# A hybrid decoder layer on one core: both token blocks of the first sub-layer multiplied before their norm factor is known

## The chip, the cores and the metric

The kernel is one program on one core of a Trainium2 chip. It has TensorE (PE, matrix products), VectorE (DVE), ScalarE (ACT), GpSimd (POOL) and SyncE (SP), each working through its own instructions in order, and DMA queues that bring data from memory. The metric is the device time of one execution in microseconds (us). The time before is the median of 3 runs, 754.89 us (753.69 to 754.94).

## The reference, cut to what matters

The layer is a SwiGLU feed-forward, a pair of token mixers and another feed-forward, each with a norm before and behind it. The change is in the first norm and in the first products that follow it:

```python
def rmsnorm(x, g):
    y = x * lax.rsqrt(jnp.mean(x * x, axis=-1, keepdims=True) + EPS)
    return y * g

def swiglu(x, w_gate, w_up, w_down):
    return (jax.nn.silu(x @ w_gate) * (x @ w_up)) @ w_down

h = x                                     # (1, 256, 1024) float32
h = h + 0.5 * rmsnorm(swiglu(rmsnorm(h, ffn1_pre_g), ffn1_w_gate, ffn1_w_up, ffn1_w_down), ffn1_post_g)
...                                       # mixers, second feed-forward
```

The norm's factor r = rsqrt(mean(x²) + eps) is one number per token. So (x·r·g) @ W = r·((x·g) @ W): the product can be made of x·g alone and multiplied by r behind it.

## The kernel before, in words

**Tiles.** The 256 tokens are two blocks of 128, block 0 and block 1; `h[:, b, halves[q]]` is half q (512 channels) of block b. Every float32 operand is split into a high part (rounded to the matrix unit's float32r) and a low remainder, and a product takes three matmuls: high·high, low·high, high·low. ACT makes the high part (for weights the cast at L167) and DVE the remainder (L168). Weights come in chunks of 1 MB, `raw`, three buffers deep (`RAW_BUFS`), loaded from SP by `load_to` (L140). `split_steps` (L150) makes `whi` and `wlo` of a chunk in two halves, then asks for a later chunk. The first feed-forward's chunks 0 and 1 are the first 512 columns of the gate weights (channels 0 to 511 and 512 to 1023), chunks 2 and 3 the same of the up weights; from chunk 4 on, 256 columns each are taken with the weights as the moving side, and both blocks at once (`mm_w`, L206).

**The opening.** `Norm.products` (L484) takes the first four chunks with the tokens standing: one token block, one chunk, 12 matmuls of 512 columns (`mm_nat`, L222), so 8 such sets, 96 matmuls. A set needs the block's activations turned to channels on partitions: PE transposes four 128x128 pieces into `pu` (`turn`, L336), ACT writes the high part times the gain (L343), DVE the remainder (L345).

- Block 0 is turned without r (`raw_u`), since r0 isn't known yet. Its products get r0 at their eviction (L527, L531), and `rescale` (L513) later makes r0·u for the rest of the sub-layer: `rescaled` (L381) spreads r0 over the partitions with a matmul of `ones` by a diagonal (`rb`, L385; the diagonal is made by POOL, L378), ACT copies it (`rbs`, L387), DVE multiplies `pu` by it (`us`, L392, 8 instructions), ACT and DVE split the result (L191, L192).
- Block 1 is normed first: DVE makes its sums of squares (L364), POOL its factor r1 (L330, L331) and x·r1 (`un`, L373), and PE turns that (`turn1`). Its products need no factor.

**Order.** Up to the end of `products` the order on PE, ACT, DVE and SP is that of the program text (`own_order(PE, ACT, DVE, SP)`, L264; POOL follows its own text). What stands between two sets is in the table `at` (L610): a number n names what is issued after the n-th set. The sets run block 0 on chunks 0 and 1, block 1 on chunks 0 and 1, block 0 on 2 and 3, block 1 on 2 and 3. `more` takes one more chunk, that is, it puts that chunk's four splitting instructions into ACT's and DVE's queues; `settle` issues the evictions held back; `rescale` stands after set 5. `norm.turns1` (block 1's turning) stands after set 1. The transposition of the block's gated product (`back`, L533) goes after set 7 for block 0 and behind set 8 for block 1. SP issues the four quarter-loads of x (256 KB each), then chunk 0 in four pieces, chunks 1 and 2 in two each, and each later chunk when a `raw` buffer is free. `warm(n)` (L291) issues n idle matmuls; 6 stand at the very start and 8 (`FILL`) ahead of the first set.

Of the kernel before, what the change touches and what calls it, by code (L numbers as in the profile page):

```python
# [36 lines left out]
RAW_BUFS = 3  # L37
AHEAD = 3
WARM = 6
FILL = 8  # L40
TAIL = 3
BG_US = 3.15
GATE_US = 1.35
# [5 lines left out]
def tile_hybrid_layer(ctx: ExitStack, tc: tile.TileContext, x, ffn1_pre_g, ffn1_w_gate, ffn1_w_up,  # L49
# [10 lines left out]
    def k4(shape, name, dt=F32):  # L60
        return sb.tile(shape, dt, tag="k4", name=name, bufs=K4_BUFS)
# [13 lines left out]
    def pj(name):  # L75

        return ps.tile([P, 512], F32, tag="pj", name=name, bufs=3)
# [62 lines left out]
    def load_to(n):  # L140
        while len(raws) < min(n, len(chunks)):
            i = len(raws)
            src, shape = chunks[i]
            r = sb.tile(shape, F32, tag="raw", name=f"raw{i}", bufs=RAW_BUFS)
            nj = shape[1] // 4 if i == 0 else shape[1] // 2 if i < 4 else shape[1]
            for j in range(0, shape[1], nj):
                nc.sync.dma_start(r[:, j:j + nj, :], src[:, j:j + nj, :])
            raws.append(r)

    def split_steps(ahead=True):  # L150


        i = len(splits)
        load_to(i + 1)
        r, shape = raws[i], chunks[i][1]
        nj = shape[1] // 2
        his, los = [], []
        splits.append((his, los))
        for q in range(2):
            hi = k4([P, nj, shape[2]], f"whi{i}{q}", F32R)  # L160
            lo = k4([P, nj, shape[2]], f"wlo{i}{q}", F32R)
            his.append(hi)
            los.append(lo)
            n = 1 if i == 0 else nj
            for j in range(0, nj, n):
                js = slice(j, j + n)
                nc.scalar.copy(hi[:, js, :], r[:, q * nj + j:q * nj + j + n, :])  # L167
                nc.vector.tensor_sub(lo[:, js, :], r[:, q * nj + j:q * nj + j + n, :], hi[:, js, :].bitcast(F32))  # L168
                yield
        raws[i] = None  # L170
        if ahead:
            load_to(i + 1 + RAW_BUFS)
# [7 lines left out]
    def take(ahead=AHEAD):  # L180

        i = taken[0]
        taken[0] += 1
        split_to(i + ahead)
        his, los = splits[i]
        splits[i] = None
        nj = chunks[i][1][1] // 2
        return (lambda j: his[j // nj][:, j % nj, :], lambda j: los[j // nj][:, j % nj, :])

    def split(hi, lo, src):  # L190
        nc.scalar.copy(hi, src)  # L191
        nc.vector.tensor_sub(lo, src, hi.bitcast(F32))  # L192
# [26 lines left out]
            nc.scalar.copy(dst[:, m, :], acc[:, T:])  # L219
            nc.vector.tensor_tensor(dst[:, m, :], acc[:, :T], dst[:, m, :], ALU.add)  # L220

    def mm_nat(acc, w, act, k0, first, last, late):  # L222


        (wh, wl), (ah, al) = w, act
        pairs = [(ah, wh), (al, wh), (ah, wl)] if late == "w" else [(ah, wh), (ah, wl), (al, wh)]
        terms = [(p, j) for j in range(4) for p in pairs[:2]] if late == "w" else \
            [(p, j) for p in pairs[:2] for j in range(4)]
        terms += [(pairs[2], j) for j in range(4)]
        for i, ((a, b), j) in enumerate(terms):  # L230
            nc.tensor.matmul(acc, a(k0 + j), b(j), start=first and i == 0, stop=last and i == 11)  # L231


    act_since, act_fence = [], [None]
# [37 lines left out]
    for b in range(2):  # L272
        for q in range(2):
            nc.sync.dma_start(h[:, b, halves[q]], xv[:, b, halves[q]])
    load_to(RAW_BUFS)
    act_table(SILU)

    ident = const.tile([P, P], F32, name="ident")
# [54 lines left out]
        return r  # L333

    last_pool = [None]
    def turn(b, q, src, g, to, name):  # L336

        pu = bg([P, 4, P], f"pu_{name}{b}{q}")
        for i in range(4):
            nc.tensor.transpose(pu[:, i, :], src[:, i * P:(i + 1) * P], ident)  # L340
        hi, lo = to(q)
        for i in range(4):
            nc.scalar.activation(hi[:, i, :], pu[:, i, :], AF.Identity, scale=g(q * 4 + i))  # L343
        for i in range(4):
            nc.vector.scalar_tensor_tensor(lo[:, i, :], pu[:, i, :], g(q * 4 + i), hi[:, i, :].bitcast(F32),  # L345
                                           ALU.mult, ALU.subtract)
        return pu

    def in_u(b):
        bs = slice(b * P, (b + 1) * P)  # L350
        return lambda q: (uT[q][:, :, 0, bs], uT[q][:, :, 1, bs])

    def of_block(to):

        parts = [to(q) for q in range(2)]
        return lambda j: parts[j // 4][0][:, j % 4, :], lambda j: parts[j // 4][1][:, j % 4, :]

    def rms(b, tag, eng=None):

        ss = tiny(2, f"ss_{tag}{b}")  # L360
        for q in range(2):
            src = h[:, b, halves[q]]
            if eng is nc.vector:
                nc.vector.scalar_tensor_tensor(jk([P, 512], f"sq_{tag}{b}{q}"), src, 1.0 / D, src, ALU.mult,  # L364
                                               ALU.mult, accum_out=ss[:, q:q + 1])
            else:
                sum_sq(ss[:, q:q + 1], src, 1.0, f"sq_{tag}{b}{q}")
        return rstd_of(ss, 1.0, f"r_{tag}{b}")

    def unit(b, q, r, tag, eng):  # L370

        un = k2([P, 512], f"un_{tag}{b}{q}")
        eng.tensor_scalar(un, h[:, b, halves[q]], r, None, ALU.mult)  # L373
        return un

    def diag(r, tag):
        dr = k2([P, P], f"dr_{tag}")
        last_pool[0] = nc.gpsimd.tensor_scalar(dr, ident, r, None, ALU.mult).ins  # L378
        return dr

    def rescaled(pus, r, g, tag, dr):  # L381

        dr = diag(r, tag) if dr is None else dr
        rb = bg([P, P], f"rb_{tag}")
        nc.tensor.matmul(rb, ones, dr, start=True, stop=True)  # L385
        rbs = k2([P, P], f"rbs_{tag}")
        nc.scalar.copy(rbs, rb)  # L387
        out = []
        for q in range(2):
            us = k2([P, 4, P], f"us_{tag}{q}")  # L390
            for i in range(4):
                nc.vector.scalar_tensor_tensor(us[:, i, :], pus[q][:, i, :], g(q * 4 + i), rbs, ALU.mult,  # L392
                                               ALU.mult)
            out.append(us)
        return out

    def set_u(us):
        for q in range(2):
            split(*in_u(0)(q), us[q])

    def post_norm(b, acc, pg, fold, tag):

# [55 lines left out]
    class Norm:  # L458

        def __init__(self, tag, g):
            self.tag, self.g, self.pus = tag, g, []
            new_u(tag)
            self.to0 = in_u(0)
            self.dr = None
            self.left = []

        def block0(self):
            for q in range(2):  # L470
                self.turn0(q)
            self.r0 = rms(0, self.tag)

        def turn0(self, q):
            self.pus.append(turn(0, q, h[:, 0, halves[q]], self.g, self.to0, self.tag))

        def unit1(self, engs=(nc.vector, nc.vector)):
            r = rms(1, self.tag)
            self.un = [unit(1, q, r, self.tag, engs[q]) for q in range(2)]

        def turn1(self, q):
            turn(1, q, self.un[q], self.g, in_u(1), self.tag)

        def products(self, ws, evict, at, turns=((0, 0), (0, 1), (1, 0), (1, 1)), late="u"):  # L484

            n = 0
            for b, i in turns:
                act = of_block(self.to0 if b == 0 else in_u(1))  # L490
                acc = pj(f"pn_{self.tag}{b}{i}")
                for c in range(2):
                    mm_nat(acc, ws[2 * i + c], act, c * 4, c == 0, c == 1, late if b == 0 else "u")
                    n += 1
                    for f in at.get(n, ()):
                        f()
                if b == 1:
                    evict(b, i, acc, None)
                else:
                    self.left.append(lambda i=i, acc=acc: evict(0, i, acc, self.r0))  # L500
            free_order()

        def turns1(self):
# [6 lines left out]
                f()  # L510
            self.left.clear()

        def rescale(self):  # L513
            set_u(rescaled(self.pus, self.r0, self.g, self.tag, self.dr))

    def ffn(post_v, tag, norm, ready, turned, then, at, ws=None, **kw):
        gu = []
# [47 lines left out]
        mm_n(acc, gu, done, turned)  # L565


    norm = Norm("f1", lambda j: cols_f[:, j:j + 1])
    raw_u = [k4([P, 4, 2, P], f"raw_u{q}", F32R) for q in range(2)]
    norm.to0 = lambda q: (raw_u[q][:, :, 0, :], raw_u[q][:, :, 1, :])  # L570
    norm.r0 = rms(0, "f1")
    r1 = rms(1, "f1", nc.vector)
    norm.un = [unit(1, q, r1, "f1", nc.gpsimd) for q in range(2)]
    norm.dr = diag(norm.r0, "f1")
    norm.turn0(0)
    for _ in split_steps(False):
        pass
    norm.turn0(1)
    warm(FILL)
    load_to(1 + RAW_BUFS)  # L580

# [11 lines left out]
    def next_norm(tag, name):  # L593
# [589 lines left out]
```

## Time and profile before

| what | value |
|---|---|
| median of 3 runs | 754.89 us |
| profiled execution, its time | 754.68 us |
| its span in the profile | 753.0 us |
| granted TensorE clock, mean | 0.998 |
| ACT busy | 437.4 us (58%) |
| DVE busy | 521.5 us (69%) |
| HBM read | 136.17 MB |

All times below count from the start of the span. In a row of the timeline stand start, duration, engine, line, operation, output and input, and the count of like instructions that were merged; what is in brackets is the idle time ahead of it and the event that ended it. A row's duration runs to the end of the last of its instructions, which overlaps the start of the next row on that engine by some tens of nanoseconds; the distance between two starts is what an instruction costs its queue. In the chain of waits each piece has its start, its share of time, engine and line.

### The profile page before, as it was taken

How to read it: one execution, taken by the hardware profiler on the slowest of the kernel's cores; microseconds unless marked ns; L12 is line 12 of the kernel's file. 1: busy time of each engine (PE TensorE's matmuls, PEld its weight loads, DVE VectorE, ACT ScalarE, POOL GpSimd, SP SyncE). 2: the span in 40 equal slices, each digit the busy share in tenths (PEclk: the TensorE clock that was granted, in tenths of full speed). 3: DMA queues.
4: the chain of work that ended last, by engine and by line, in shares of the span. 5: the costliest groups of instructions: out<-in, count | busy, mean ns of one | idle time of the engine just before them, and what ended most of it. 6: DMA issues, size and time to landing. Idle time of an engine off the chain costs nothing.

```text
span 753.0 us, 11051 instructions
## 1 busy us (share of the span) xinstructions
PE 743.3 (99%) x4377; PEld 645.6 (86%) x4377; DVE 521.5 (69%) x790; ACT 437.4 (58%) x732; POOL 40.0 (5%) x76
## 2 busy tenths in 40 slices
PE   8999999999999999999999999999999999999996
PEld 6888888888889999898999778788888888888885
DVE  6685567664577888767778987695684867766612
ACT  7475556553565565858856556783563746564511
POOL 6400000000200000000000000000010000000000
PEclk9999999999999999999999999999999999999999
DMA  8685776486253647565555454466361677545701
GB/s 314 151 275 168 224 224 238 164 297 223 64 167 115 188 149 224 171 201 182 175 168 190 165 205 138 141 227 249 111 228 53 224 224 224 169 179 186 276 1 56
DMA packets 94212, 137.96 MB, mean 183 GB/s; under 512 B 2684, under 2 KB 68304, under 8 KB 94160
## 3 DMA queue, kind: packets, MB, share of 16 engines
q1 hardware_dynamic: 91488, 129.51, 52.2%
q0 software_dynamic: 2368, 7.22, 3.1%
q8 instruction: 34, 0.56, 0.3%
q10 hardware_dynamic: 304, 0.53, 0.2%
q14 instruction: 18, 0.15, 0.1%
HBM read 136.17 MB, written 1.08 MB: 182 GB/s over the span
## 4 chain that ended last, share of the span: by engine, by line
PE 96%; DVE 1%; POOL 1%; DMA 1%; ACT 1%; issue 0%; SPq 0%; DVEq 0%; POOLq 0%; ACTq 0%
PE acc_f L433 16%; PE pup_f L216 9%; PE pg_f L216 9%; PE pws L231 6%; PE pgt L231 6%; PE pn_f L231 5%; PE pg_f L215 4%; PE pup_f L215 4%; PE acc_mx L433 3%; PE pn_mx L231 3%; PE pwd L231 3%; PE pxs L204 2%; PE pxs L202 2%; PE pxs L201 2%; PE pz L204 2%; PE pz L201 2%
## 5 line engine op out<-in xcount | busy, mean ns | idle before, releaser
L168 DVE TENSOR_TENSOR wlo<-raw,whi 128x1024 fp32r<-128x1024 f32 (+1 forms) x246 | 291.5, 1214 | 56.3 <-ACT whi L167 53.6
L167 ACT CAST whi<-raw 128x1024 fp32r<-128x1024 f32 (+1 forms) x246 | 247.3, 1044 | 59.4 <-PE acc_f L433 16.7
L216 PE MATMUL pg_f<-u_f,whi 128*128 128x512 f32 x288 | 101.2, 396 | 0.0
L216 PE MATMUL pup_f<-u_f,whi 128*128 128x512 f32 x288 | 101.1, 396 | 0.0
L215 PE MATMUL pg_f<-u_f,wlo 128*128 128x256 f32 x252 | 70.5, 280 | 0.0
L215 PE MATMUL pup_f<-u_f,wlo 128*128 128x256 f32 x252 | 70.3, 279 | 0.0
L216 PEld LDWEIGHTS pg_f<-u_f,whi 128*128 128x128 f32 x288 | 52.9, 188 | 9.8
L216 PEld LDWEIGHTS pup_f<-u_f,whi 128*128 128x128 f32 x288 | 52.7, 188 | 9.8
L433 PE MATMUL acc_f<-whi,gh_f 128*128 128x512 f32 x176 | 58.2, 390 | 0.0
L433 PE MATMUL acc_f<-whi,gl_f 128*128 128x512 f32 x176 | 58.1, 389 | 0.0
L433 PE MATMUL acc_f<-wlo,gh_f 128*128 128x512 f32 x176 | 58.0, 389 | 0.0
L215 PEld LDWEIGHTS pg_f<-u_f,wlo 128*128 128x128 f32 x252 | 47.5, 189 | 1.7
L215 PEld LDWEIGHTS pup_f<-u_f,wlo 128*128 128x128 f32 x252 | 47.5, 189 | 1.6
L220 DVE TENSOR_TENSOR su_f<-pup_f,su_f 128x256 f32<-128x256 f32 x36 | 15.2, 423 | 38.7 <-ACT su_f L219 38.7
L433 PEld LDWEIGHTS acc_f<-whi,gl_f 128*128 128x128 f32 x176 | 33.0, 188 | 6.9
L433 PEld LDWEIGHTS acc_f<-wlo,gh_f 128*128 128x128 f32 x176 | 33.0, 188 | 6.9
L433 PEld LDWEIGHTS acc_f<-whi,gh_f 128*128 128x128 f32 x176 | 33.0, 188 | 6.7
L231 PE MATMUL pgt<-whi,u_mx 128*128 128x512 f32 x128 | 34.8, 400 | 0.0
L201 PE MATMUL pz<-u_mx,whi 128*128 128x256 f32 x128 | 32.3, 288 | 0.0
L202 PE MATMUL pz<-u_mx,whi 128*128 128x256 f32 x128 | 31.8, 284 | 0.0
L201 PE MATMUL pxs<-u_mx,whi 128*128 128x256 f32 x128 | 31.7, 285 | 0.0
L202 PE MATMUL pxs<-u_mx,whi 128*128 128x256 f32 x128 | 31.4, 283 | 0.0
(315 smaller groups left out, 1423.9 us busy)
## 6 DMA issues: line engine op xcount, KB each, us to landing
raw<-in_w_in_dram SPq DMA_DIRECT2D x40, 1024.0 KB, 5.3
raw<-in_ffn_w_down_dram SPq DMA_DIRECT2D x22, 1024.0 KB, 5.4
raw<-in_ffn_w_gate_dram SPq DMA_DIRECT2D x20, 1024.0 KB, 5.7
raw<-in_ffn_w_up_dram SPq DMA_DIRECT2D x20, 1024.0 KB, 5.8
raw<-in_ssd_w_branch_dram SPq DMA_DIRECT2D x8, 1024.0 KB, 5.1
acb<-acd POOLq DMA_DIRECT2D x8, 512.0 KB, 4.8
raw<-in_da_w_branch_dram SPq DMA_DIRECT2D x4, 1024.0 KB, 5.2
raw<-in_w_out_dram SPq DMA_DIRECT2D x4, 1024.0 KB, 4.8
```

The costliest lines, as they stand in the source:

```text
L167: nc.scalar.copy(hi[:, js, :], r[:, q * nj + j:q * nj + j + n, :])
L168: nc.vector.tensor_sub(lo[:, js, :], r[:, q * nj + j:q * nj + j + n, :], hi[:, js, :].bitcast(F32))
L201: nc.tensor.matmul(acc[m], wh(j)[:, cs], ah(k0 + j), start=first and j == ks[0], stop=False)
L202: nc.tensor.matmul(acc[m], wh(j)[:, cs], al(k0 + j), start=False, stop=False)
L204: nc.tensor.matmul(acc[m], wl(j)[:, cs], ah(k0 + j), start=False, stop=last and j == ks[-1])
L215: nc.tensor.matmul(acc[:, :T], wl(j)[:, cs], ah(j), start=False, stop=False)
L216: nc.tensor.matmul(acc, wh(j)[:, cs], ahl(j), start=j == 0, stop=j == KD - 1)
L220: nc.vector.tensor_tensor(dst[:, m, :], acc[:, :T], dst[:, m, :], ALU.add)
L231: nc.tensor.matmul(acc, a(k0 + j), b(j), start=first and i == 0, stop=last and i == 11)
L433: nc.tensor.matmul(acc[b][q], x_[:, ts], w_(kt)[:, halves[q]], start=i == 0 and kt == 0 and x_ is ah and w_ is wh, stop=i == n - 1 and kt ...
```

## The change

- Block 1 is also turned without its factor (`raw=(0, 1)`): its transposes read `h` as loaded, its products are evicted with r1, and a second `rescale(1)` makes r1·u later. `raw_u` has four tiles in place of two. POOL's `un` and DVE's sums of squares are gone; r1 comes from ACT's sums of squares (`second`), and the second diagonal is made by DVE.
- Chunk 0 is loaded between block 0's and block 1's halves of x (`load_to((1, RAW_BUFS)[b])`).
- The sets run in another order: block 0 on chunk 0, block 1 on chunk 0, block 0 on 1, block 1 on 1, then block 0 on 2 and 3, block 1 on 2 and 3. The first set has an order of its own ("q"), with block 1's transposes behind its 10th and its 12th matmul (`between`).
- `turn` is cut in two: `transposed` (PE) and `gained` (ACT and DVE). Block 0's second half is gained only after the first set. `ws` starts with one chunk; `more` stands after sets 1, 3 and 4, `rescale(0)` after set 3, `rescale(1)` after set 5.
- `FILL` goes from 8 to 2.

```diff
-FILL = 8
+FILL = 2
...
-    def mm_nat(acc, w, act, k0, first, last, late):
+    def mm_nat(acc, w, act, k0, first, last, late, between={}):
...
+        if late == "q":
+            js = [[(ah, wh, j), (al, wh, j)] for j in range(4)]
+            ls = [[(ah, wl, j)] for j in range(4)]
+            terms = js[0] + js[1] + ls[0] + js[2] + ls[1] + js[3] + ls[2] + ls[3]
+        elif late == "w":
+            terms = [(a, wh, j) for j in range(4) for a in (ah, al)] + [(ah, wl, j) for j in range(4)]
+        else:
+            terms = [(a, b, j) for a, b in ((ah, wh), (ah, wl), (al, wh)) for j in range(4)]
+        for i, (a, b, j) in enumerate(terms):
             nc.tensor.matmul(acc, a(k0 + j), b(j), start=first and i == 0, stop=last and i == 11)
+            if i + 1 in between:
+                between[i + 1]()
...
     for b in range(2):
         for q in range(2):
             nc.sync.dma_start(h[:, b, halves[q]], xv[:, b, halves[q]])
-    load_to(RAW_BUFS)
+        load_to((1, RAW_BUFS)[b])
...
-    def diag(r, tag):
+    def diag(r, tag, eng=nc.gpsimd):
         dr = k2([P, P], f"dr_{tag}")
-        last_pool[0] = nc.gpsimd.tensor_scalar(dr, ident, r, None, ALU.mult).ins
+        f = eng.tensor_scalar(dr, ident, r, None, ALU.mult)
...
+            for n, (b, i, c, late) in enumerate(turns or [(b, i, c, "u") for b in range(2) for i in range(2)
+                                                          for c in range(2)]):
+                if c == 0:
+                    accs[b, i] = pj(f"pn_{self.tag}{b}{i}")
+                acc = accs[b, i]
+                mm_nat(acc, ws[2 * i + c], of_block(self.to[b]), c * 4, c == 0, c == 1, late,
+                       {} if n else between)
+                if c == 1 and b in self.raw:
+                    self.left.append(lambda b=b, i=i, acc=acc: evict(b, i, acc, self.r[b]))
+                elif c == 1:
                     evict(b, i, acc, None)
-                else:
-                    self.left.append(lambda i=i, acc=acc: evict(0, i, acc, self.r0))
+                for f in at.get(n + 1, ()):
+                    f()
+            self.settle()
             free_order()
...
-    norm = Norm("f1", lambda j: cols_f[:, j:j + 1])
-    raw_u = [k4([P, 4, 2, P], f"raw_u{q}", F32R) for q in range(2)]
-    norm.to0 = lambda q: (raw_u[q][:, :, 0, :], raw_u[q][:, :, 1, :])
-    norm.r0 = rms(0, "f1")
-    r1 = rms(1, "f1", nc.vector)
-    norm.un = [unit(1, q, r1, "f1", nc.gpsimd) for q in range(2)]
-    norm.dr = diag(norm.r0, "f1")
+    norm = Norm("f1", lambda j: cols_f[:, j:j + 1], (0, 1))
+    raw_u = [[k4([P, 4, 2, P], f"raw_u{b}{q}", F32R) for q in range(2)] for b in range(2)]
+    norm.to = [lambda q, b=b: (raw_u[b][q][:, :, 0, :], raw_u[b][q][:, :, 1, :]) for b in range(2)]
+    norm.r[0] = rms(0, "f1")
+    norm.dr[0] = diag(norm.r[0], "f10")
     norm.turn0(0)
+    norm.raised(0, 1)
     for _ in split_steps(False):
         pass
-    norm.turn0(1)
     warm(FILL)
     load_to(1 + RAW_BUFS)
...
-    ws = [take(1) for _ in range(2)]
+    ws = [take(1)]
     more = lambda: ws.append(take(1))
+
+    def second():
+
+        norm.r[1] = rms(1, "f1")
+        norm.dr[1] = diag(norm.r[1], "f11", nc.vector)
+
...
-        {1: [norm.turns1], 2: [more], 4: [norm.settle, more], 5: [norm.rescale], 7: [norm.settle, None]}, ws,
-        turns=((0, 0), (1, 0), (0, 1), (1, 1)), late="w")
+        {1: [lambda: norm.gained(1, 0), lambda: norm.gained(0, 1), more], 2: [lambda: norm.gained(1, 1), second],
+         3: [more, lambda: norm.rescale(0)], 4: [norm.settle, more], 5: [lambda: norm.rescale(1)],
+         7: [norm.settle, None]}, ws,
+        turns=[(0, 0, 0, "q"), (1, 0, 0, "u"), (0, 0, 1, "w"), (1, 0, 1, "u"), (0, 1, 0, "w"), (0, 1, 1, "w"),
+               (1, 1, 0, "u"), (1, 1, 1, "u")],
+        between={10: lambda: norm.raised(1, 0), 12: lambda: norm.raised(1, 1)})
     norm = made[0]
```

More of the change, by code (lines that the diff above doesn't have):

```diff
@@ L458, in tile_hybrid_layer, with __init__ @@
     class Norm:
-        def __init__(self, tag, g):
-            self.tag, self.g, self.pus = tag, g, []
+        def __init__(self, tag, g, raw=(0,)):
+            self.tag, self.g, self.raw = tag, g, raw
             new_u(tag)
-            self.to0 = in_u(0)
-            self.dr = None
+            self.to = [in_u(b) for b in range(2)]
+            self.pus, self.r, self.dr = [[], []], [None, None], [None, None]
             self.left = []
@@ L471, in block0, with raised, gained @@
                 self.turn0(q)
[L472 removed]
+            self.r[0] = rms(0, self.tag)
         def turn0(self, q):
[L475 removed]
+            self.raised(0, q)
+            self.gained(0, q)
+        def raised(self, b, q):
+            self.pus[b].append(transposed(b, q, h[:, b, halves[q]], self.tag))
+        def gained(self, b, q):
+            gained(self.pus[b][q], q, self.g, self.to[b])
         def unit1(self, engs=(nc.vector, nc.vector)):
```

37 lines of the change are left out of this document (15 added, 22 removed).

## The prediction, made before the changed kernel ran

> **What bounds the kernel now.** I read the page first (busy times, chain that ended last), then the chain in order of time over the opening, a table of stages, and the timeline of each engine up to 36 us, since the diff touches nothing behind that.
>
> ```profile
> PE 743.3 (99%) x4377; PEld 645.6 (86%) x4377; DVE 521.5 (69%) x790; ACT 437.4 (58%) x732; POOL 40.0 (5%) x76
> PE 96%; DVE 1%; POOL 1%; DMA 1%; ACT 1%; issue 0%; SPq 0%; DVEq 0%; POOLq 0%; ACTq 0%
> ```
>
> TensorE is busy from its first product to the end, and the chain is 96% TensorE. So the opening's worth is one number: when PE reaches the first `mm_w` product (`pg_f`, L216). Whatever that start moves by, the end moves by.
>
> ```profile
> 14.06 10.92 PE pn_f L231 x48
> 24.98 0.22 PE rb_f L385 x2
> 25.20 5.46 PE pn_f L231 x24
> 30.66 0.44 PE pt_f L537 x4
> ...
> 8.58 2.71 PE L231 MATMUL pn_f<-whi,raw_u 128*128 128x512 f32 x8 [0.37 <-ACT whi L167]
> 33.71 0.62 PE L216 MATMUL pg_f<-u_f,whi 128*128 128x512 f32 x2
> ...
> 0.00:8.58 8.58, 6.62 (x38) 6.18 (x38) 2.10 (x8) 4.42 (x11) 2.10 (x13) 1.00 0.73 236
> 8.58:16.43 7.85, 7.35 (x32) 4.95 (x33) 7.85 (x17) 7.65 (x18) 7.74 (x6) 1.00 1.05 393
> 21.87:33.49 11.62, 11.62 (x56) 9.63 (x55) 5.59 (x13) 4.46 (x7) 5.14 (x14) 1.00 0.76 181
> ```
>
> In the chain a matmul costs 10.92/48 = 0.2275 us, so a set of 12 costs 2.73 and the eight sets 21.84. PE needs 33.71 - 8.58 = 25.13 for them, that is 3.3 for transposes and waits. The stage rows (after stretch and length: PE, PEld, DVE, ACT, POOL, granted clock, DMA share, GB/s) show where the slack is: from 8.58 to 16.43 DVE and ACT are as full as PE (7.85 and 7.65 of 7.85), and only from 21.87 on have they half their time free. A change that puts more on them before that point pays for it.
>
> **The change, part by part.** First the start.
>
> ```profile
> 0.80 1.79 SPq L274 DMA_DIRECT2D h<-in_x_dram  x4
> 2.63 3.68 SPq L147 DMA_DIRECT2D raw<-in_ffn_w_gate_dram  x6
> 6.18 0.69 DVE L364 SCALAR_TENSOR_TENSOR sq_f<-h 128x512 f32<-128x512 f32 x1 [1.26 <-DMA h<-in_x_dram]
> 7.35 0.69 DVE L364 SCALAR_TENSOR_TENSOR sq_f<-h 128x512 f32<-128x512 f32 x1 [0.47 <-DMA h<-in_x_dram]
> ...
> 3.77 0.63 ACT L325 ACTIVATE sq_f<-h 128x512 f32<-128x512 f32 x1 [1.07 <-DMA h<-in_x_dram]
> 5.80 1.15 ACT L343 ACTIVATE raw_u<-pu_f,cols_f 128x128 fp32r<-128x128 f32 x4 [0.69 <-PE pu_f L340]
> 7.91 2.59 ACT L167 CAST whi<-raw 128x512 fp32r<-128x512 f32 x4 [0.96 <-DMA raw<-in_ffn_w_gate_dram]
> 10.40 1.14 ACT L343 ACTIVATE raw_u<-pu_f,cols_f 128x128 fp32r<-128x128 f32 x4
> 11.42 2.21 ACT L167 CAST whi<-raw 128x1024 fp32r<-128x1024 f32 x2
> 17.43 0.74 ACT L245 ACTIVATE sg_f1b<-pn_f,r_f 128x512 f32<-128x512 f32 x1
> 18.02 2.05 ACT L167 CAST whi<-raw 128x1024 fp32r<-128x1024 f32 x2
> ```
>
> SP issues the same pieces of 256 KB; chunk 0's four take the places of block 1's halves (landed 6.18 and 7.35, where DVE's waits end) and of its own first two (7.91 and one cast, 0.65, later). ACT is through with `raw_u` at 5.80 + 1.02 (the step from 10.40 to 11.42) = 6.82, so four casts at 0.65 (2.59/4) run from 6.82 to 9.4, and PE starts at 7.5 in place of 8.58: **1.1 us won**. If the pieces land in the new places no earlier than before, this is 0. Block 1's halves now land about 9.2 and 9.8, ahead of their transposes. The casts pace PE as before, so set 1's 10th matmul ends near 9.95; transposes (0.44 for four, as `pt_f`), two matmuls, transposes: 11.3. The 6 lost warm matmuls stood in PE's wait and cost nothing themselves.
>
> Now what is queued on ACT, DVE and POOL behind that.
>
> ```profile
> 7.97 1.12 DVE L345 SCALAR_TENSOR_TENSOR raw_u<-pu_f,cols_f,raw_u 128x128 fp32r<-128x128 f32 x4
> 9.01 2.91 DVE L168 TENSOR_TENSOR wlo<-raw,whi 128x512 fp32r<-128x512 f32 x4
> 17.20 4.62 DVE L168 TENSOR_TENSOR wlo<-raw,whi 128x1024 fp32r<-128x1024 f32 x4
> 25.54 2.16 DVE L392 SCALAR_TENSOR_TENSOR us_f<-pu_f,cols_f,rbs_f 128x128 f32<-128x128 f32 x8 [3.71 <-ACT rbs_f L387]
> 27.62 1.47 DVE L192 TENSOR_TENSOR u_f<-us_f,u_f 128x512 fp32r<-128x512 f32 x2
> 29.00 0.75 DVE L531 SCALAR_TENSOR_TENSOR sg_f1b<-pn_f,r_f,sg_f1b 128x512 f32<-128x512 f32 x1
> 26.70 0.62 ACT L191 CAST u_f<-us_f 128x512 fp32r<-128x512 f32 x1 [1.19 <-DVE us_f L392]
> ...
> 5.21 0.30 POOL L330 TENSOR_SCALAR r_f<-ss_f 128x1 f32<-128x1 f32 x1 [3.67 <-ACT sq_f L325]
> 5.59 0.57 POOL L331 TENSOR_TENSOR r_f<-r_f,nhalf 128x1 f32<-128x1 f32 x1
> 9.21 4.15 POOL L373 TENSOR_SCALAR un_f<-h,r_f 128x512 f32<-128x512 f32 x2
> 13.41 0.66 PE L340 MATMUL pu_f<-ident,un_f 128*128 128x128 f32 x4 [0.50 <-POOL un_f L373]
> ```
>
> *Removed:* DVE's two squares (1.4 us, ahead of 8.1) and POOL's `un` (4.15). Both stood beside the DMA and the casts; PE waited for `un` by 0.50 at 13.41, which goes. *Added:* two squares on ACT (1.3), a diagonal on DVE and a second `rescale` (2.08 of `us`, 1.4 of L192 on DVE, 1.5 on ACT). *Moved:* the first `rescale`, from behind all four chunks' splitting to ahead of chunk 3's. Prices per step: four L343, 1.02 on ACT; four L345, 1.04 on DVE; a 1024 cast 1.02; a 1024 `wlo` 1.155 (4.62/4); eight `us` 2.08 (25.54 to 27.62); L531 0.75.
>
> ACT goes in program order: block 1's first half 10.6 to 11.6 (behind its transposes), block 0's second half to 12.6, chunk 1's casts to 14.7, block 1's second half to 15.7, the squares to 17.0. POOL's r1 takes 0.95 (5.21 to 6.16): 18.05. **DVE's diagonal waits for that**, and behind it in DVE's queue stand chunk 2's `wlo` and the whole first `rescale`. The diagonal has no row on DVE; between nothing and a `us` step of 0.26 (2.08/8, the same shape with one operand more) I take 0.26. Then `wlo` 18.3 to 20.7 and `us` to 22.8. ACT casts the second half of u to 23.4, makes two silus (0.59 each, 17.43 to 18.02) to 24.65, and only then, next in its queue, **casts chunk 3: first half 25.7**, second 26.7. The `wlo` of chunk 3 follow at 26.9 and 28.05.
>
> PE meanwhile: set 2 from 11.3 to 14.0; set 3 (paced by chunk 1's second `wlo`, 14.7 + 1.5 = 16.2) to 16.75; `rb` 0.22; set 4 to 19.7; set 5 to 22.4, `rb` to 22.65. Set 6 needs chunk 3: **it waits from 22.65 to 25.7, 3.05 us**, and ends at 28.6. Set 7 ends at 31.3. The transposes behind it wait for L531, in DVE's queue behind the second `rescale`: 28.05 + 2.08 + 0.7 (its casts) + 0.7 + 0.75 = 32.25, **0.95 us more**. With 0.44 and set 8, `pg_f` starts at 35.4.
>
> Sum: start -1.1, waits +3.05 and +0.95, the four transposes and one more `rb` against those of before and their small waits -1.2: 35.4 against 33.7, **+1.7 us**. Chunk 4's casts then follow the transposes' copy as they did before, so the shift stays as it is. As 0.05 of hand-over was left out at some ten steps of the ACT-DVE chain, half of them hidden, I take +1.8: 754.7 + 1.8 = 756.5 on the profiled execution; that one lies 0.2 under the median, so **756.6** for a median. The ends: the ACT and DVE steps between 10.6 and 25.7 (15 us) 5% shorter take 0.8 off the first wait and 0.3 off the second: +0.7; 5% longer: +2.9. If the start brings nothing, ACT's chain starts 1.1 later and so does all behind it: +2.9.
>
> **Rivals.**
>
> *The clock drops in the wait.* PE would idle 3.05 us, longer than anywhere in this trace behind the start. What it costs shows at the start:
>
> ```profile
> 1.59 2.93 PE L294 MATMUL warm<-ident 128*128 128x128 f32 x12 [1.59 <-POOL ident L280]
> 4.65 1.77 PE L340 MATMUL pu_f<-ident,h 128*128 128x128 f32 x8
> ```
>
> Eight transposes take 1.77, 0.2 each, against 0.11 in `pt_f`; half speed lasted from 1.59 to about 6.1. Another 4.5 us at half speed loses 2.25: 758.9. Against it: the matmuls paced by casts (0.37 waits) kept the granted clock at 1.00. The Trainium skill, "TensorE: Matmul & The Clock Gate", Part 1 (the HAM clock gate), says that the array falls to half its clock after an idle window of about 3.4 us. By that rule the wait is just too short, unless it comes out 0.4 longer; no wait in this trace tests it.
>
> *The wait is shorter.* DVE's `wlo` of 512 ran beside POOL's `un` at 0.73 (2.91/4); L192 of that size cost the same 0.73 (1.47/2) without it, so little is to be had there. But every hand-over that I placed late shortens it, and at two thirds of the wait the sum is +0.8 or less: 755.5, no change to be told.
>
> *PE never starves (faster).* The mechanism: chunk 3's first cast is done before set 6 asks. Then the start's 1.1, the vanished `un` wait 0.5 and the transposes tucked into set 1 remain: 7.5 + 21.84 + transposes and `rb` 1.8 = 31.1 to 31.7, with the second wait gone too: -2.3, 752.4. It decides at 22.65: the cast must be 3.05 earlier. For it speaks POOL, 4 us lighter; against it, that ACT's queue holds chunk 3 behind u's casts, and DVE's squares and `us` aren't removed but grown.
>
> **How the numbers follow.** Forecast (wait of 2 to 4 us) 0.55, clock 0.13, shorter wait 0.20, never starves 0.12. A measurement of this kernel tells about 0.2%, 1.5 us, from no change: slower begins at 756.4. The forecast's own range 755.9 to 757.8 has a small part (0.07) under that. Slower 0.48 + 0.13 = 0.61, no change 0.07 + 0.20 = 0.27, faster 0.12. The range leaves out the fast case and some of the clock's tail: 754.9 to 759.0.
>
> **What would show it.** The first `pn_f` near 7.5; on PE, a wait before set 6 put down to ACT's `whi` and of about 3 us, and one of about 1 before the first `pt_f`, put down to DVE; on DVE, a wait for POOL's r before the diagonal near 17.3; the first `pg_f` near 35.4; behind that, each row late by the same. I am wrong if set 6 finds its cast done, if the granted clock falls below 1.00 behind 22 us, or if PE waits again after `pg_f`.

## The result, and the profile after

The changed kernel takes 756.67 us (756.41 to 757.07, 8 runs) where the kernel before takes 754.91 beside it (753.69 to 755.04, 8 runs): a ratio of 1.0027, 95% interval 1.0018 to 1.0035, so a slowdown that is small but clear of the spread. The profiled executions, 756.41 and 754.68, lie 1.73 apart, and so do their spans, 754.7 and 753.0. The forecast was 756.6.

The page of the changed kernel: busy time and instructions of each engine, then the shares of the chain that ended last.

```profile
PE 742.6 (98%) x4367; PEld 645.0 (85%) x4367; DVE 524.0 (69%) x797; ACT 440.4 (58%) x739; POOL 34.7 (5%) x74
PE 94%; DVE 2%; ACT 2%; issue 0%; POOL 0%; DVEq 0%; POOLq 0%; ACTq 0%
```

POOL is lighter by 5 us, ACT and DVE are each heavier by 2 to 3. TensorE does no more than before (742.6 us busy for 743.3); its share of the chain fell from 96% to 94%, and ACT's and DVE's grew from 1% to 2% each. So work of theirs now stands between two pieces of TensorE's. The waits of TensorE in the changed kernel (us in total, times, the longest) say where:

```profile
PE pn_f L236 <- ACT whi L167: 2.5, 1, 2.5
...
PE pt_f L564 <- DVE sg_f1b L558: 0.7, 1, 0.7
```

The waits of 0.5 and 0.4 in the old opening are gone, and these two have come, 2.5 for a weight cast and 0.7 for a gated product. TensorE's timeline in the changed kernel has both in place:

```profile
7.50 1.27 PE L236 MATMUL pn_f<-whi,raw_u 128*128 128x512 f32 x4
...
10.24 0.60 PE L346 MATMUL pu_f<-ident,h 128*128 128x128 f32 x4
...
11.50 1.17 PE L236 MATMUL pn_f<-whi,raw_u 128*128 128x512 f32 x4
...
22.81 0.39 PE L402 MATMUL rb_f<-dr_f,ones 128*128 128x128 f32 x2
25.73 2.18 PE L236 MATMUL pn_f<-whi,raw_u 128*128 128x512 f32 x8 [2.54 <-ACT whi L167]
...
30.52 1.07 PE L236 MATMUL pn_f<-whi,raw_u 128*128 128x512 f32 x4
32.24 0.66 PE L564 MATMUL pt_f<-ident,sg_f1b 128*128 128x128 f32 x4 [0.66 <-DVE sg_f1b L558]
...
35.49 0.61 PE L216 MATMUL pg_f<-u_f,whi 128*128 128x512 f32 x2
```

The first product starts at 7.50 instead of 8.58, and the first `pg_f` at 35.49 instead of 33.71: 1.08 won at the start, 1.78 lost at the end of the opening. Between the two starts TensorE needs 27.99 where it needed 25.13. By the distances of starts the first wait is 2.70 (two `rb` matmuls from 22.81 at 0.22, so 23.03 to 25.73) and the second 0.81 (set 7's last four matmuls from 30.52 at 0.2275, so 31.43 to 32.24).

Why the cast came at 25.7 is in three timelines of the changed kernel, those of POOL, DVE and ACT in this order:

```profile
17.69 0.57 POOL L338 TENSOR_TENSOR r_f<-r_f,nhalf 128x1 f32<-128x1 f32 x1
```

```profile
18.30 0.29 DVE L393 TENSOR_SCALAR dr_f<-ident,r_f 128x128 f32<-128x128 f32 x1 [0.78 <-POOL r_f L338]
18.50 2.36 DVE L168 TENSOR_TENSOR wlo<-raw,whi 128x1024 fp32r<-128x1024 f32 x2
20.78 2.16 DVE L409 SCALAR_TENSOR_TENSOR us_f<-pu_f,cols_f,rbs_f 128x128 f32<-128x128 f32 x8
...
27.99 2.16 DVE L409 SCALAR_TENSOR_TENSOR us_f<-pu_f,cols_f,rbs_f 128x128 f32<-128x128 f32 x8
...
31.45 0.74 DVE L558 SCALAR_TENSOR_TENSOR sg_f1b<-pn_f,r_f,sg_f1b 128x512 f32<-128x512 f32 x1
```

```profile
21.93 0.62 ACT L191 CAST u_f<-us_f 128x512 fp32r<-128x512 f32 x1 [2.68 <-DVE us_f L409]
22.96 0.62 ACT L191 CAST u_f<-us_f 128x512 fp32r<-128x512 f32 x1 [0.41 <-DVE us_f L409]
23.49 1.26 ACT L252 ACTIVATE sg_f1b<-pn_f,r_f 128x512 f32<-128x512 f32 x2
24.64 1.99 ACT L167 CAST whi<-raw 128x1024 fp32r<-128x1024 f32 x2
```

Read them from the bottom. ACT casts chunk 3 from 24.64, right behind two silus (the activation of the gate products), which stand behind the two casts of u, for which ACT waited 2.68 and 0.41 on DVE's `us`. `us` stands behind chunk 2's `wlo`, and that behind the diagonal, for which DVE had waited 0.78 on POOL's r1. Chunk 3's cast needs none of them; it only stands behind them in ACT's queue, even in the 2.68 in which ACT does nothing. The second wait has the same form. L558 is the eviction of block 0's product with chunks 2 and 3, which set 6 finished at 28.7, but it is issued after set 7, and so it stands behind the second `us` and its splitting in DVE's queue.

Behind `pg_f` nothing is new. The first products of the later stages start 1.72 or 1.73 later than before, each of those looked at (the up weights at 41.90 for 40.17, the mixers' products at 197.80 for 196.07, the end of the span at 754.71 for 752.98).

### The profile page after: what moved, and what is told of

Same layout as the page of the kernel before. It is cut to its first block, busy times and chain, and to the rows that moved or that the text cites. A ratio compares the mean times of both kernels' runs of the same rounds, so it can differ in the third digit from the quotient of the medians.

```text
span 754.7 us, 11039 instructions
## 1 busy us (share of the span) xinstructions
PE 742.6 (98%) x4367; PEld 645.0 (85%) x4367; DVE 524.0 (69%) x797; ACT 440.4 (58%) x739; POOL 34.7 (5%) x74
## 3 DMA queue, kind: packets, MB, share of 16 engines
HBM read 136.17 MB, written 1.08 MB: 182 GB/s over the span
## 4 chain that ended last, share of the span: by engine, by line
PE 94%; DVE 2%; ACT 2%; issue 0%; POOL 0%; DVEq 0%; POOLq 0%; ACTq 0%
PE acc_f L450 16%; PE pg_f L216 9%; PE pup_f L216 9%; PE pws L236 6%; PE pgt L236 6%; PE pg_f L215 4%; PE pup_f L215 4%; PE pn_f L236 4%; PE acc_mx L450 3%; PE pn_mx L236 3%; PE pwd L236 3%; PE pxs L204 2%; PE pxs L202 2%; PE pxs L201 2%; PE pz L204 2%; PE pz L201 2%
## 5 line engine op out<-in xcount | busy, mean ns | idle before, releaser
L219 ACT COPY su_f<-pup_f 128x256 f32<-128x256 f32 x36 | 13.4, 371 | 31.9 <-PE pup_f L216 31.8
L201 PE MATMUL pxs<-u_mx,whi 128*128 128x256 f32 x128 | 31.7, 285 | 0.0
```

The lines of the kernel that those rows point to most:

```text
L201: nc.tensor.matmul(acc[m], wh(j)[:, cs], ah(k0 + j), start=first and j == ks[0], stop=False)
```

## The experiments

Each edit is made in the changed kernel unless it says otherwise. The kernel before ran beside each; its medians there lay between 754.32 and 754.77. Since it moves by that much from one set of runs to the next, small distances are better read from the ratios and from the profiles than from the medians.

**The evictions behind the cast.** Chunk 3's splitting goes into the queues ahead of the two silus.

```diff
-         3: [more, lambda: norm.rescale(0)], 4: [norm.settle, more], 5: [lambda: norm.rescale(1)],
+         3: [more, lambda: norm.rescale(0)], 4: [more, norm.settle], 5: [lambda: norm.rescale(1)],
```

> Changed kernel, the two silus (settle) issued behind chunk 3's splitting in place of ahead of it. Theory A (PE's wait ahead of set 6 hangs on what stands in ACT's queue ahead of chunk 3's first cast): the cast comes up by what the silus cost there, 24.64 - 23.49 = 1.15 us in the changed kernel's rows, the wait falls from 2.5 to about 1.4, the wait for DVE ahead of pt_f stays, the first pg_f stands at 34.4, time 756.7 - 1.1 = 755.6. Theory B (the wait is the landing of chunk 3's data or the clock, not the queue): no change, 756.7.

Measured: 755.27 us (754.9 to 755.42, 11 runs), ratio 1.0012 (1.0003 to 1.0021). Its timeline of ACT, then of TensorE:

```profile
23.49 1.99 ACT L167 CAST whi<-raw 128x1024 fp32r<-128x1024 f32 x2
25.38 1.25 ACT L252 ACTIVATE sg_f1b<-pn_f,r_f 128x512 f32<-128x512 f32 x2
```

```profile
24.58 2.15 PE L236 MATMUL pn_f<-whi,raw_u 128*128 128x512 f32 x8 [1.38 <-ACT whi L167]
...
31.18 0.65 PE L564 MATMUL pt_f<-ident,sg_f1b 128*128 128x128 f32 x4 [0.64 <-DVE sg_f1b L558]
...
34.42 0.62 PE L216 MATMUL pg_f<-u_f,whi 128*128 128x512 f32 x2
```

The two silus' 1.15 came off the wait, 1.07 off `pg_f` (35.49 to 34.42) and, by the two ratios (1.0027 and 1.0012), about 1.1 off the time; the medians lie 1.4 apart. The queue order is what the wait hangs on; the silus are still done, only later.

**The first `rescale` behind chunk 3 as well.**

```diff
-         3: [more, lambda: norm.rescale(0)], 4: [norm.settle, more], 5: [lambda: norm.rescale(1)],
+         3: [more], 4: [more, norm.settle, lambda: norm.rescale(0)], 5: [lambda: norm.rescale(1)],
```

> Changed kernel, first rescale and silus behind chunk 3's splitting (rescale of block 0 after set 4, of block 1 after set 5 as it was). Theory A: the wait ahead of set 6 goes altogether, but both rescales now stand in DVE's queue ahead of the multiplication that the transposes behind set 7 wait for, so that wait grows from 0.7 to about 2.9; first pg_f near 34.0, time 755.2, between the changed kernel and the kernel before. Theory B (only the first wait costs; the work behind it catches up): the whole 2.5 come back, 754.0. Theory C (the wait isn't of this order): 756.7.

Measured: 756.24 us (754.85 to 756.54, 11 runs), ratio 1.0018 (1.0009 to 1.0027). The median is a miss, and the runs say why: they are two groups, five from 754.85 to 754.92, each with a mean granted clock of 0.998, and six from 756.24 to 756.54, each with 0.995 or 0.996. The profiled execution, 756.53, is of the upper group:

```profile
30.73 0.66 PE L564 MATMUL pt_f<-ident,sg_f1b 128*128 128x128 f32 x4 [2.06 <-DVE sg_f1b L558]
31.15 1.86 PE L236 MATMUL pn_f<-whi,raw_u 128*128 128x512 f32 x4
32.81 1.91 PE L236 MATMUL pn_f<-wlo,raw_u 128*128 128x512 f32 x4
...
35.57 0.63 PE L216 MATMUL pg_f<-u_f,whi 128*128 128x512 f32 x2
```

The first wait is gone. TensorE now comes early to its transposes and waits 2.06 for L558, which stands as far back in DVE's queue as before. Behind that wait four matmuls take 1.86 and the next four 1.91, where in the changed kernel they took 1.17 and 1.08. A table of stages of the same execution (from and to, length, busy time of PE, PEld, DVE, ACT and POOL, granted clock, DMA share, GB/s) shows the cause:

```profile
27.96:31.37 3.41, 1.35 (x9) 0.89 (x8) 2.63 (x6) 0.92 (x2) 1.98 (x4) 1.00 0.76 84
31.37:34.79 3.42, 3.42 (x10) 2.64 (x9) 1.92 (x2) 3.36 (x4) 0.00 (x0) 0.50 0.43 14
```

Behind a stretch in which TensorE was busy 1.35 of 3.41 us the granted clock was 0.50 for as long again.

**The same, with the idle time filled.** The first eight matmuls of set 7 are issued twice; this work is repeated and computes nothing new.

```diff
+        if late[0] == "d":
+            late = late[1:]
+            for i in range(8):
+                nc.tensor.matmul(acc, (ah, al)[i % 2](k0 + i // 2), wh(i // 2), start=i == 0, stop=i == 7)
...
-               (1, 1, 0, "u"), (1, 1, 1, "u")],
+               (1, 1, 0, "du"), (1, 1, 1, "u")],
```

> The kernel with the first rescale behind chunk 3's splitting, with the first 8 matmuls of set 7 issued twice in the same way: 1.8 us of the wait of 2.4 us ahead of pt_f are filled with work. Without the filling its runs lay at 754.85 to 754.92 (granted clock 0.998) or at 756.24 to 756.54 (0.995 to 0.996). Theory A (the idle time makes the clock fall for one stretch of 3.4 us, which costs 1.6): all runs near 754.9. Theory B (the two groups have another cause): two groups again, or 756.5 and more.

Measured: 754.87 us (754.36 to 755.16, 12 runs), ratio 0.9997 (0.9988 to 1.0007). One group, at the place of the lower one. TensorE's timeline:

```profile
30.75 0.66 PE L568 MATMUL pt_f<-ident,sg_f1b 128*128 128x128 f32 x4 [0.28 <-DVE sg_f1b L562]
31.16 1.17 PE L240 MATMUL pn_f<-whi,raw_u 128*128 128x512 f32 x4
...
33.99 0.61 PE L216 MATMUL pg_f<-u_f,whi 128*128 128x512 f32 x2
```

The transposes start where they did (30.75 for 30.73), since L558 sets them; the four matmuls behind them are back at full speed, and `pg_f` is 1.58 earlier. 1.8 us of useless work took 1.4 off the median: the upper group was the clock's.

**The changed kernel again, and with its own wait filled.** The first ran without an edit, the second with the first eight matmuls of set 5 issued twice (the same lines as above, with "dw" in that set's place).

> The changed kernel as it is, beside the next two on one chip. In its profiled run the clock held through the wait of 2.5 us; in four of its eight runs the granted clock was 0.996 and not 0.998, which is what one stretch of 3.4 us at half speed costs (3.4 x 0.5 / 755 = 0.002). Theory A (the wait costs a clock drop in some executions; its 1.7 us are partly taken out of the second wait of 0.7 to 1.0): 756.4 to 757.1 again, the runs of lower clock 0.3 to 0.7 us longer. Theory B (the clock differs only at the start): no tie between clock and time.

> Changed kernel with the first 8 matmuls of set 5 issued twice (the first time into the same accumulator, which is then started afresh, so nothing changes in the values): 1.8 us more work on PE, all of it in the time that it waits ahead of set 6, which leaves a wait of 0.7 us. Theory A (clock drops because of that wait): no drop behind 20 us in the profile, and no run of lower clock and longer time: all near 756.4. Theory B (more work on PE costs time): 758.2.

Measured: 756.55 us (756.42 to 757.04, 12 runs), ratio 1.0024 (1.0014 to 1.0034), and 756.38 (756.08 to 756.54, 12 runs), ratio 1.0016 (1.0006 to 1.0027). The profiled execution of the first shows a fall of the clock that the one above doesn't. Its stages, TensorE's timeline and a row of DVE's:

```profile
21.99:25.40 3.41, 0.90 (x6) 0.59 (x5) 1.91 (x6) 3.00 (x6) 3.41 (x10) 1.00 0.95 308
25.40:28.82 3.42, 3.42 (x8) 2.74 (x9) 3.42 (x7) 1.06 (x2) 2.57 (x6) 0.50 0.24 17
```

```profile
25.40 3.68 PE L236 MATMUL pn_f<-whi,raw_u 128*128 128x512 f32 x8 [2.51 <-ACT whi L167]
...
32.55 0.60 PE L564 MATMUL pt_f<-ident,sg_f1b 128*128 128x128 f32 x4
...
35.73 0.62 PE L216 MATMUL pg_f<-u_f,whi 128*128 128x512 f32 x2
```

```profile
31.20 0.75 DVE L558 SCALAR_TENSOR_TENSOR sg_f1b<-pn_f,r_f,sg_f1b 128x512 f32<-128x512 f32 x1
```

The wait is the same, 2.51 for 2.54, yet here the clock fell behind it. Eight matmuls took 3.5 to the next row's start in place of 2.0, but `pg_f` is only 0.24 later than in the first profile: the second wait has gone (no bracket at 32.55), so the drop went mostly into time in which TensorE would have waited for L558. L558 was through at about 31.9 here, so of the drop some 0.6 was felt, and 0.3 of that was covered by this execution's earlier start. With the wait filled, the profile shows no drop and `pg_f` at 35.44, and no run lies above 756.54. The medians' distance, 0.17, is small against the spread, and the two intervals overlap. Of the twelve runs without filling, the four with a mean clock of 0.998 lie at 756.42 to 756.52, the eight with a lower one at 756.43 to 757.04. But the execution whose drop is on record took 756.57, so what put three runs at 757.01 to 757.04 is not shown.

**Chunk 3 and both evictions ahead of the `rescale`s.** The queues of ACT and DVE in the order in which TensorE asks: chunk 3's splitting, the silus, then `rescale(0)`; block 0's L558 ahead of `rescale(1)`.

```diff
-         3: [more, lambda: norm.rescale(0)], 4: [norm.settle, more], 5: [lambda: norm.rescale(1)],
-         7: [norm.settle, None]}, ws,
+         3: [more], 4: [more, norm.settle, lambda: norm.rescale(0)], 6: [norm.settle, lambda: norm.rescale(1)],
+         7: [None]}, ws,
```

> Changed kernel in another order: chunk 3 split right after set 4, then silus and the rescale of block 0; after set 6 the evictions (block 0's multiplication first), then the rescale of block 1. Theory A (all of the loss is queue order): PE waits nowhere between set 1 and the first pg_f, which stands at 31.6 to 31.8; the splitting of chunks 4 and 5 is then the next to be late, and some 0.7 to 0.9 is given back at pg_f; time 753.5 to 754.0, faster than both kernels. Theory B (DVE and ACT are the bound of the opening whatever the order: their added work has to be paid): 755.5 or more.

Measured: **753.53 us** (753.41 to 753.68, 11 runs), ratio 0.999 (0.9981 to 0.9999): faster than both kernels, 0.8 under the median of the kernel before beside it (754.32). TensorE's timeline:

```profile
28.43 0.60 PE L564 MATMUL pt_f<-ident,sg_f1b 128*128 128x128 f32 x4
...
31.61 0.61 PE L216 MATMUL pg_f<-u_f,whi 128*128 128x512 f32 x2
...
32.62 0.66 PE L564 MATMUL pt_f<-ident,sg_f1b 128*128 128x128 f32 x4 [0.39 <-DVE sg_f1b L558]
...
33.75 0.38 PE L218 MATMUL pg_f<-u_f,wlo 128*128 128x256 f32 x1 [0.28 <-DVE wlo L168]
```

And a row of ACT's, the casts of chunks 2 and 3:

```profile
16.94 3.96 ACT L167 CAST whi<-raw 128x1024 fp32r<-128x1024 f32 x4
```

Behind the first product no row of the eight sets has a bracket any more, nor have the transposes at 28.43, and the mean clock is 0.999. ACT casts chunk 3 right behind chunk 2, without a wait and through by 20.9, so its data is there some five microseconds before the changed kernel casts it at 24.64: the wait for the cast isn't one for the load. `pg_f` starts 2.10 earlier than before the change; 1.17 of that is left at the up weights (39.00 for 40.17), since TensorE now waits 0.39 and 0.28 for what DVE has put off. Every instruction that the change added is in this kernel too, so their work isn't what the change costs; where they stand in the queues is.

**The second diagonal on POOL.**

```diff
-        norm.dr[1] = diag(norm.r[1], "f11", nc.vector)
+        norm.dr[1] = diag(norm.r[1], "f11")
```

> Changed kernel, block 1's diagonal made by POOL (0.63 us there in the changed kernel) and not by DVE. Theory A: DVE no longer stands still for POOL's r ahead of chunk 2's remainder (0.78 us idle, 0.2 of work); part of that is lost again to ACT's copy of the spread factor, so the wait ahead of set 6 falls by 0.4 to 0.9: time 755.8 to 756.3. Theory B (DVE's standstill lies in the shade of ACT's queue, which is full there): no change, 756.7.

Measured: 756.7 us (756.2 to 756.86, 6 runs), ratio 1.0029 (1.0018 to 1.0041). A miss. DVE no longer waits for r1 but now waits 0.65 for ACT's cast of chunk 2, so `wlo` starts at 18.14 for 18.50 and set 6 only 0.36 earlier; in the profiled execution the clock then falls. POOL's timeline, TensorE's (eight matmuls take 3.1 to the next row's start at half clock for most of them), and the stage that holds the wait:

```profile
18.32 2.58 POOL L393 TENSOR_SCALAR dr_f<-ident,r_f 128x128 f32<-128x128 f32 x1
```

```profile
25.37 3.29 PE L236 MATMUL pn_f<-whi,raw_u 128*128 128x512 f32 x8 [2.22 <-ACT whi L167]
```

```profile
22.56:25.97 3.41, 1.19 (x7) 0.87 (x6) 1.92 (x4) 3.37 (x5) 3.41 (x9) 1.00 0.84 280
```

So the wait for POOL's r1 is a link of the chain in the profile, but ACT's queue stands close behind it, and what it gives back is too little to show in the time.

**The first `rescale` made twice.** The second time repeats work.

```diff
-         3: [more, lambda: norm.rescale(0)], 4: [norm.settle, more], 5: [lambda: norm.rescale(1)],
+         3: [more, lambda: norm.rescale(0), lambda: norm.rescale(0)], 4: [norm.settle, more], 5: [lambda: norm.rescale(1)],
```

> Changed kernel, the first rescale issued twice (the same values written again), a doubled suspected cost. Theory A: DVE and ACT get 3.5 us more ahead of chunk 3's cast, so the first pg_f is 3.5 late, near 39, time 760.2, with the wait on PE split between the second spreading matmul and set 6. Theory B (clock): with an idle stretch of 4 us or more ahead of set 6 the granted clock falls to half for some us behind it, and the time is 2 us over that, 762. Theory C (the rescale isn't on the path): 756.7 to 757.

Measured: 760.05 us (759.89 to 760.6, 5 runs), ratio 1.0071 (1.0059 to 1.0084): 3.4 to 3.5 above the changed kernel. What stands on ACT and DVE ahead of chunk 3's cast is paid in full: in the profile the cast starts at 28.15 for 24.64 and set 6 at 29.24 for 25.73, 3.51 later each. A wait of 1.8 for the copied factor has come in front of the second `rb`, and the clock falls twice, at 20.39 and at 30.63; the profiled execution, 760.6, is the slowest of the five, with `pg_f` 4.18 later (39.67).

**The weights behind all of x again, in the changed kernel.**

```diff
     for b in range(2):
         for q in range(2):
             nc.sync.dma_start(h[:, b, halves[q]], xv[:, b, halves[q]])
-        load_to((1, RAW_BUFS)[b])
+    load_to(RAW_BUFS)
```

> Changed kernel, the loads in the order of before (all of x, then chunk 0). Theory A (the new load order wins 1.1 us at the start, and the whole ACT-DVE chain starts from there): first pn_f at 8.6 in place of 7.5, everything behind it 1.1 later, time 757.8. Theory B (the start isn't on the path, since set 6 waits anyway for the chain behind the squares of block 1, whose data would come earlier): 756.7.

Measured: 758.44 us (757.35 to 759.51, 5 runs), ratio 1.0047 (1.0034 to 1.0059). TensorE's timeline:

```profile
9.08 1.40 PE L236 MATMUL pn_f<-whi,raw_u 128*128 128x512 f32 x4 [1.60 <-ACT whi L167]
...
37.59 0.62 PE L216 MATMUL pg_f<-u_f,whi 128*128 128x512 f32 x2
```

ACT waits 1.46 for the weights, and the first product starts 1.58 later. The wait at set 6 is still there, 2.5 long, and set 6 starts 1.47 later (27.20 for 25.73). In this execution the clock falls behind that wait as well (0.50 from 27.97 to 31.38), and `pg_f` is 2.10 later; so of the 1.8 between the medians, and of `pg_f`'s distance, a part is the clock's. All five runs lie above every run of the changed kernel. The early load is worth about what the start shows, and a wait further on didn't swallow it.

**The early load alone, in the kernel before.**

```diff
-    load_to(RAW_BUFS)
+        load_to((1, RAW_BUFS)[b])
```

> Kernel before with the new load order alone (chunk 0 between the halves of x). Theory A (the order pays only together with the unnormed block 1): DVE's squares of block 1 stand ahead of everything else in its queue and now wait for data that lands at 9.2 and 9.8, so block 0's remainders and with them the second matmul come at 11.2 in place of 8.9, and POOL's un is late too; first pg_f 2.7 late, time 757.6. Theory B (the earlier weights win 1.1 us by themselves): 753.8.

Measured: 757.37 us (757.19 to 758.09, 5 runs), ratio 1.0036 (1.0024 to 1.0049). DVE's timeline and TensorE's:

```profile
9.12 0.69 DVE L364 SCALAR_TENSOR_TENSOR sq_f<-h 128x512 f32<-128x512 f32 x1 [4.20 <-DMA h<-in_x_dram]
```

```profile
10.82 2.75 PE L231 MATMUL pn_f<-whi,raw_u 128*128 128x512 f32 x7 [3.02 <-DVE raw_u L345]
```

TensorE starts at 7.32 and stops after one matmul: DVE's squares of block 1 stand in its queue ahead of block 0's `raw_u` remainder, and block 1 now lands later. Behind this wait, too, the clock falls: TensorE is busy 0.77 of the 3.41 us up to 11.59, and the clock is 0.50 from there to 15.00. How much of the loss is the clock's was not separated. `pg_f` starts at 36.17 for 33.71. So the same load order costs 2.5 there where DVE makes block 1's norm and gains where block 1 is multiplied without it.

**Eight filling matmuls as before.**

```diff
-FILL = 2
+FILL = 8
```

> Changed kernel with 8 warm matmuls in place of 2 ahead of set 1. The 6 more cost 6 x 0.223 = 1.34 us of PE's queue, of which 0.7 to 0.9 lie in its wait for the first cast: first pn_f near 8.0. Theory A (set 1 is paced by casts and the chain by block 1's transposes): the transposes move by 0.2 to 0.4, time 756.9 to 757.1. Theory B (fewer warm matmuls keep the clock at half for longer, seen as granted clocks of 0.996 in half of the changed kernel's runs): with 8 the clock is up earlier, set 1 and the sets behind it gain, time 756.3 or less.

Measured: 757.27 us (756.54 to 757.7, 7 runs), ratio 1.003 (1.0019 to 1.0041). TensorE's timeline:

```profile
6.42 2.35 PE L301 MATMUL warm<-ident 128*128 128x128 f32 x16
8.52 1.18 PE L236 MATMUL pn_f<-whi,raw_u 128*128 128x512 f32 x4
```

With the early load the fill no longer stands in a wait: it ends at 8.5, a microsecond behind the first cast. The first product is 1.0 late, block 1's transposes (10.91 for 10.24) and set 6 (26.40 for 25.73) are 0.67 late, more than theory A said. In this profile, the slowest of the seven runs, the clock falls behind the wait at set 6 (0.50 from 27.73 to 31.15), and `pg_f` is 1.3 late (36.80). The gain of theory B did not come. By the time alone the cost isn't clear: the interval overlaps that of the changed kernel.

## Why the prediction was right, and which steps were off

The forecast, +1.8 with the two waits, came out: +1.78 at `pg_f` and +1.73 in time. (By its own terms, 756.5 and 0.2, the median would be 756.7 rather than the 756.6 written; 756.67 was measured.) By its own steps:

- *The start:* 7.5 predicted, 7.50 seen. Its alternative, that the pieces land no earlier, is out, and the load put back took 1.5 away again at set 6.
- *Lost warm matmuls cost nothing:* nothing speaks against it. Put back, they stand in the way by 0.67 at set 6.
- *The ACT-DVE chain:* squares at 17.0, r1 at 18.05, chunk 3's first cast at 25.7, L558 done at 32.25. Seen: ACT through at 17.02, r1 at 18.26, set 6 at 25.73, L558 done at 32.19 and the transposes at 32.24. The diagonal's unknown price of 0.26 is a step of 0.20, and chunk 2's `wlo` took 2.28 for 2.4; that these made good most of r1's 0.2 is luck.
- *TensorE's way to set 6 was mis-sized.* It was to be there at 22.65, so the wait at 3.05; it came at 23.03 and the wait is 2.70. The terms that failed are set 1, whose transposes came at 10.24 for 9.95, so that set 2 started at 11.50 for 11.3, and set 3, which waits for chunk 1's second `wlo`: that ended at 16.48 for 16.2, and set 3 at 17.11 for 16.75. Since chunk 3's cast ends the wait anyway, the error cost nothing: a slower TensorE only waits less.
- *The second wait:* 0.95 predicted, 0.81 seen: TensorE came to it at 31.43 for 31.3, and DVE's L558 set the end of it.
- *The sum:* -1.08 + 2.70 + 0.81 = 2.43, so the third term, transposes and small waits, is -0.65 and not -1.2. The two waits were 0.49 too long, the third term 0.55 too low. That these cancel is not luck: `pg_f` comes the transposes and set 8 behind L558, whenever TensorE gets there, and L558 was placed right.
- *Behind it:* a constant shift, and no new wait.

Of the rivals, *TensorE never starves* is false for this order, but its price was near: it put `pg_f` at 31.1 to 31.7, and the reordered kernel has it at 31.61. What it left out is that `pg_f`'s own inputs are then late, so that 752.4 became 753.5. *The shorter wait* took place to a small part, 2.70 for 3.05, and gained nothing by it, since chunk 3's cast set the end of it either way.

*The clock rival* was half right. The prediction held the wait to be too short for it, 0.4 below what would be needed; waits of 1.8 to 3.0 were enough in several executions. One of its own signs of being wrong, a granted clock under 1.00 behind 22 us, thus showed in one of the two profiles of the changed kernel. And the price, 2.25 from 4.5 us at half speed, was too large: the drop lasts 3.4 us, so at most 1.7, and in this kernel most of that falls into the second wait. (The 4.5 us at the start were read from durations. They bear it out, the same warm matmul taking 0.24 from 1.59 and 0.12 from 6.25, but the stage row of 0.00 to 8.58 gives a granted clock of 1.00, so that column doesn't show the start.) In the kernel with the first `rescale` late, where no wait follows, all 1.6 of it shows. The forecast's own mechanism carries the time with and without the drop.

The cause is thus queue order: work that TensorE needs late was put ahead of work that it needs next, on two engines. For the first wait this is shown by the evictions put behind the cast and by the doubled `rescale`, for both waits by the last reordering. Not tried: block 1's squares earlier on ACT, and the reordered kernel with DVE's late steps spread so that `pg_f`'s first columns don't wait.

## What to carry to other kernels

Removing work from one engine doesn't help where what takes its place is queued ahead of something that the bound engine needs sooner: write down, for each queue, when each item is asked for, and issue in that order. Put a load earlier only together with the change that makes it the next thing needed; alone it cost 2.5 us here, the clock's part included. Where the bound engine must idle two or three microseconds, look at the clock in the rows behind the wait as well as at the wait, and over several runs.

## What the runs showed of the hardware

**The clock falls behind an idle time shorter than was expected, and on a grid.** In these traces the granted clock changes at multiples of about 3.41 us from each other (with the doubled `rescale` it falls at 20.39, is back at 23.80 and falls again at 30.63, three times 3.413 behind the first), and what goes with a fall is the busy share of the one such stretch ahead of it. Stretches in which TensorE was busy 0.90, 1.19, 1.35 of 3.41 us (the rows above) were followed by one at 0.50. The fullest that was followed by a fall is of the doubled `rescale`; the emptiest that was not, of the kernel with the weights behind all of x; and another that was not, of the changed kernel's first profile:

```profile
16.98:20.39 3.41, 1.59 (x10) 1.23 (x9) 2.63 (x6) 2.27 (x5) 3.00 (x6) 1.00 0.79 238
```

```profile
7.49:10.90 3.41, 1.82 (x7) 1.21 (x8) 2.46 (x6) 2.32 (x4) 0.00 (x0) 1.00 1.03 388
```

```profile
21.34:24.75 3.41, 1.86 (x10) 1.39 (x8) 2.88 (x9) 2.41 (x5) 3.41 (x9) 1.00 0.81 232
```

So the edge lay between 1.59 and 1.82, about half. In all thirteen traces every such stretch with 1.60 or less was followed by a fall, and none with 1.82 or more. Where no fall is near, the borders are counted back from one: 10.90 lies five times 3.4133 ahead of that execution's fall at 27.97, and 24.75 lies 213 times 3.4133 ahead of the fall at the end of the other, at 751.79. The changed kernel's wait of 2.5 fell across two stretches in that execution (23.03 to 25.73, with the border at 24.75; the clock stayed at 1.00) and whole into one in another (22.7 to 25.40, with the border there): the same kernel, the same wait, and by these two the drop comes or not by where the grid lies. The Trainium skill, "TensorE: Matmul & The Clock Gate", Part 1 (the HAM clock gate), says that the window is 3413 ns long and runs freely. The borders above bear that out, 3.413 apart and at 24.75 in one execution and 25.40 in another of the same kernel. The Trainium skill's rule, in the same part, is that idle gaps of more than about 3.4 us are to be avoided. That is not the limit seen here, where waits of 1.8 to 3.0 were followed by a fall.

**POOL's 128x128 multiply took 0.63 us alone and 2.58 beside a busy DVE.** The first diagonal, in the changed kernel, stood beside little; the second, with the diagonal on POOL, beside DVE's `wlo` (the row of 18.32 above), and so did the one of the kernel before, which took 2.35 at 13.34. That DVE is the cause was not tested; it is read from where these rows stand.

```profile
6.44 0.63 POOL L393 TENSOR_SCALAR dr_f<-ident,r_f 128x128 f32<-128x128 f32 x1
```
